# Recurrent chains in six phases a chunk that advance lane by lane in step, with TensorE's program in emission order in the second of two stretches

## The chip, the cores and the metric

The kernel runs on one core of a Trainium2 chip. The metric is the device time of one execution in microseconds (us); a smaller number is better. A profile gives for one execution each instruction's start and duration on the five engines: TensorE (PE, with its weight loads as PEld), VectorE (DVE), ScalarE (ACT), GpSimd (POOL) and SyncE (SP), which here issues nearly all DMAs.

## What is computed

One step of a hybrid backbone over 1152 tokens, 128 of context and 1024 latent, with model width 1024. A shared input projection feeds two parallel heads: a matrix-valued recurrence (RWKV-7: 8 heads of 64, both directions of time) and a gated linear recurrence (RG-LRU). Their outputs are concatenated, projected, gated and added; a gated feed-forward block with a width-3 convolution and a final norm follow. All vectors of shift, scale and gate come from a modulation product of the conditioning with `w_mod`. Cut to what the change concerns, of the reference:

```python
def _wkv7_step(S, inp):
    r_t, w_t, kk_t, b_t, k_t, v_t = inp
    sa = jnp.einsum('dbhij,dbhj->dbhi', S, kk_t)
    S = S * w_t[..., None, :] - sa[..., :, None] * b_t[..., None, :] + v_t[..., :, None] * k_t[..., None, :]
    y = jnp.einsum('dbhij,dbhj->dbhi', S, r_t)
    return S, y
...
mod = (jax.nn.silu(cvec) @ lp['w_mod'] + lp['b_mod'])[..., None, :]
...
x = x + g1 * (jnp.concatenate([ya, yb], axis=-1) @ lp['w_out'])
```

## The kernel before

**Chunks and lanes.** The matrix recurrence is done in chunks of 64 tokens. Two heads share one group f (0 to 3), and both directions of time go side by side. A chain (`chain`, L1100) carries the state of such a group through its tile positions p, two chunks (n_ = 0, 1) a position. For each chunk TensorE computes: keys and receptances times the state (KR by S, 128x128); G·V, the masked products of the chunk by the values (64x64 blocks); T·R, the triangular inverse times the right-hand side (64x64); K·V, the update of the state, and the second half of G·V (both 128x64). Between them ScalarE and VectorE copy the right-hand side R out of PSUM, write T·R into the values VS, add K·V to the state S and add the output o. `prep` (L1079) makes the next chunk's products: a 128x256 block product that VectorE masks into G (L1087), a scaling on GpSimd (L1090), and transposes (L1094) that ScalarE copies into Kt (L1095).

**Two stretches.** Four lanes carry the chains. Lanes a and b begin while the projection is still under way: the first stretch runs them beside `rest_of_projection` (L991), with the RG-LRU. Then memory is freed, and the second stretch runs the rest of a and b, lanes c and d (groups 0 and 1 from position 5 on), the normalisation of finished pieces (`post`, L1277, whose transposes are `po`), the rest of the modulation (`mod_rest`, L1335: sets of eight 128x512 tiles `wmod`, multiplied into PSUM tile `md` in 32-column pieces by `mod_part`, L315, then turned by `mod_cols`) and the RG-LRU half of the output projection (`wout_lru`, L1413: rounded weights `woh`, `wol`, products `wo`).

**Order.** `beside_all` takes its generators in proportion to given weights; the code emits instructions in that order. A scheduler then orders each engine's instructions: among those that it deems ready, the first emitted goes first. A chunk of a chain has three steps (three `yield`s). PSUM has eight banks; `deal` names the banks that a kind of product takes in turn, and a new product in a bank waits until the earlier one there has been read. For the second stretch:

```python
    two = (2, 4)
    deal(ya=(3,), yb=(5,), yc=(0,), yd=(1,), pa=two, pb=two, pc=two, pd=two, ca=two[::-1], cb=two[::-1], cc=two[::-1],
         cd=two[::-1], md=(6,), wo=(7,), po=two)
    run_all((lane_a, 98 - LA), (lane_b, 98 - LB), (lane_c, 26), (lane_d, 26), (posts(90), 90),
            (seq(mod_rest(16, 24), beside_all((mod_rest(24, 48), 30), (wout_lru(), 48))), FL))
```

Here p stands for the products of `prep`, c for T·R and K·V, y for the outputs. In the first stretch each of these has its own bank for a and for b. LA is 74, LB 52: the steps of a and b in the first stretch, 24 and 16.7 chunks.

Of the kernel before, what the change touches and what calls it, by code (L numbers as in the profile page):

```python
# [10 lines left out]
AF = mybir.ActivationFunctionType  # L11
# [6 lines left out]
NT = 9  # L18
# [3 lines left out]
SPAN = ((0, 384), (384, 768), (768, 1152))  # L22


LA = 74
NT4, NAB4, NAG, NP, NL4, NC2 = 2, 4, 10, 1, 6, 6
PK, PX, PU = 4, 2, 4
RA, RL, RI, RK = 4, 1, 3, 2
# [2 lines left out]
def beside_all(*gens):  # L31

    st = [[g, float(n), 0] for g, n in gens]
    while st:
        s = min(st, key=lambda e: e[2] / e[1])
        try:
            next(s[0])
            s[2] += 1
            yield
        except StopIteration:  # L40
            st.remove(s)

# [16 lines left out]
def tile_hybrid_step(  # L59
# [10 lines left out]
    load = nc.sync.dma_start  # L70
# [20 lines left out]
    def mm(out, lhsT, rhs, start=True, stop=True):  # L91
        PE.matmul(out, lhsT, rhs, start=start, stop=stop, skip_group_check=True)  # L92
# [25 lines left out]
    def half(i):  # L118
        return slice(64 * i, 64 * i + 64)
# [113 lines left out]
    n = 0  # L233
# [708 lines left out]
    class Background:  # L942


        def __init__(self):
            self.q, self.done = [], set()
# [5 lines left out]
        def step(self):  # L952
            if not self.q:
                return False
            try:
                next(self.q[0])
            except StopIteration:
                self.done.add(id(self.q.pop(0)))
            return True

        def finish(self, g=None):
            while self.q and (g is None or id(g) not in self.done):
                self.step()

    bg_a, bg_l, bg_i, bg_k, bg_p = [Background() for _ in range(5)]

    def beside(gens, *rates):
        credit = [0.0] * 4
# [58 lines left out]
    class Lane:  # L1027


        def __init__(self, pool, k, out=None):  # L1030
            self.out = out or pool
            self.pool, self.k, self.py, self.pc, self.pp = pool, k, "y" + k, "c" + k, "p" + k

        def ring(self, name, n, bufs=2):
            return self.pool.tile([128, n], F32, name=name, tag=name + self.k, bufs=bufs)

# [21 lines left out]
    def fetch_keys(L, q, n_):  # L1058

        cs = slice(128 * n_, 128 * n_ + 128)  # L1060
        bk = L.ring("BK", 256).rearrange("p (d t) -> p d t", d=2)
        load(bk, kb_d[q.f, q.p, :, :, 1, cs])
        if n_ == 1:
            for e in range(2):
                A.activation(L.kx[half(e), :, :, e, :], q.KR[half(e)], AF.Copy)
        q.X[n_] = bk, L.kx[:, :, n_]

    FO = 2
    WL = V
# [9 lines left out]
    def prep(L, q, n_):  # L1079

        gm = L.ring("G", 512).rearrange("p (d e t) -> p d e t", e=2, d=2)
        km = L.ring("Kt", 256)
        bk, kx = q.X.pop(n_)
        ps = bank(L.pp)
        for d in range(2):
            mm(ps[:, 256 * d:256 * d + 256], bk[:, d], kx[:, d].rearrange("p e t -> p (e t)"))
        V.tensor_tensor(gm, ps.rearrange("p (d e t) -> p d e t", e=2, d=2),  # L1087
                        mask[:, :, n_].unsqueeze(2).to_broadcast([128, 2, 2, 128]), op=OP.mult)
        x = 2 * q.p + n_
        G.tensor_tensor(bk, bk, pc_f[q.f][:, :, x:x + 1].to_broadcast([128, 2, 128]), op=OP.mult)  # L1090
        yield
        ps = bank(L.pp)
        for d in range(2):
            PE.transpose(ps[:, 128 * d:128 * d + 128], bk[:, d], ident)  # L1094
        A.activation(km, ps[:, 0:256], AF.Copy)  # L1095
        q.G[n_] = gm
        q.K[n_] = km.rearrange("p (d t) -> p d t", d=2)
        yield

    def chain(L, pairs):  # L1100

        ring, S_buf = [0], L.states()

        def next_state():
# [4 lines left out]
        qs = {0: fetch(L, *pairs[0])}  # L1109
        fetch_keys(L, qs[0], 0)  # L1110
        fetch_keys(L, qs[0], 1)
        yield from prep(L, qs[0], 0)
        Sc = None
        for hi, (i, n_) in enumerate(hops):
            f, p = pairs[i]
# [39 lines left out]
            py = bank(L.py)  # L1155
            for d in range(2):
                mm(py[:, 128 * d:128 * d + 128], q.KR[:, d, n_], Sc[:, d, :], d == 0, False)
            for e in range(2):
                for d in range(2):
                    vh = vhalf(n_, d)  # L1160
                    mm(py[half(1 - vh), 128 * d + 64 * e:128 * d + 64 * e + 64], q.G[n_][half(vh), d, e, half(1 - vh)],
                       q.V[half(vh), n_, d, half(e)], False, True)
# [10 lines left out]
            for d in range(2):  # L1173
                sh = half(1 - vhalf(n_, d))
                copy(use[d], q.V[sh, n_, d, :], ps[sh, 0:128])
            next(ahead, None)
            yield
            if not last:
                ps = bank(L.pc)
# [12 lines left out]
            for d in range(2):  # L1192
                vh = half(vhalf(n_, d))
                dst, src = o[vh] if p == 0 else o[vh, d if p < 5 else 1 - d], py[vh, 128 * d:128 * d + 128]
                if p > 4 or (p == 0 and n_ == 1):
                    V.tensor_tensor(dst, src, dst, op=OP.add)
                else:
                    A.activation(dst, src, AF.Copy)
            for _ in ahead:
                pass  # L1200
            yield
            if p == 0 and n_ == 1:
                ctx_final(L, f, Sc)
                if f % 2:
                    bg_p.push(late_post(None, f // 2, oX))
            elif p > 4 and n_ == 1:
                bg_p.push(late_post(f, p, o))
            elif n_ == 1:
                spill(o_d[f, 4 - p], o.rearrange("p d c -> p (d c)"))
                if p == 4 and (i + 1 == len(pairs) or pairs[i + 1] != (f, 5)):  # L1210
                    spill(s_d[f], Sc.rearrange("p d c -> p (d c)"))

    def late_post(f, p, o):
        yield from post(f, p, o)
# [10 lines left out]

    oX = rp.tile([128, 512], F32, name="oX")
    E, LATE = range(1, 5), range(5, NT)
    lane_a = chain(Lane(rp, "a"), [(0, p) for p in E] + [(f, 0) for f in range(4)] + [(2, p) for p in range(1, NT)])
    lane_b = chain(Lane(rp, "b"), [(1, p) for p in E] + [(3, p) for p in range(1, NT)])

    PB = 2
    TM = 3
# [3 lines left out]
    YB = 2  # L1236
    YS = 1
    XP = 2
    FL = 88
    XC = 3  # L1240
    OC = 3
    OB = 3
    LB = 52

    def take(g, n):
        for _ in range(n):
            next(g)
            yield

    run_all((take(lane_a, LA), LA), (take(lane_b, LB), LB), (rest_of_projection(), 12 + (54 - 6 * len(EARLY)) * 4 // PK))  # L1250
    ph.close()
    use[1] = A
    pqs = ExitStack()
# [8 lines left out]
    def of_output(name):  # L1262
        return pw if name in ("woh", "wol", "yb", "ybh", "ybl") else p3

    lane_c, lane_d = [chain(Lane(lcd, k, pq), [(f, p) for p in LATE]) for f, k in ((0, "c"), (1, "d"))]

    def p2(name, dt=F32, bufs=2):
        return of_output(name).tile([128, 512], dt, name=name, tag=name, bufs=bufs)
# [57 lines left out]
            spill(y_d[2 * p:2 * p + 2, :, 0:128].rearrange("f p t -> p f t"), gt)  # L1326
        yield

    def posts(n):
        for _ in range(n):  # L1330
            bg_p.step()
            yield


    def mod_rest(i0, i1):  # L1335
        for idx in range(i0, i1, 4):
            ps = bank("md")
            raw = []
            for k in range(8):
                raw.append(p2("wmod", bufs=6))  # L1340
                load(raw[k], ins["w_mod"][0, 128 * k:128 * k + 128, 128 * idx:128 * idx + 512])
                if k % 2:
                    yield
                if k % 4 == 3:
                    for i in range(k - 3, k + 1):
                        mod_part(ps, slice(0, 512), i, raw[i], True)
            row = p2("tm")
            A.activation(row, ps, AF.Copy)
            mod_cols(idx, row, 4)
            yield  # L1350

# [61 lines left out]
    def wout_lru():  # L1413
# [24 lines left out]
        for k in range(4):  # L1438
# [3 lines left out]
    two = (2, 4)  # L1442
    deal(ya=(3,), yb=(5,), yc=(0,), yd=(1,), pa=two, pb=two, pc=two, pd=two, ca=two[::-1], cb=two[::-1], cc=two[::-1],
         cd=two[::-1], md=(6,), wo=(7,), po=two)
    run_all((lane_a, 98 - LA), (lane_b, 98 - LB), (lane_c, 26), (lane_d, 26), (posts(90), 90),
            (seq(mod_rest(16, 24), beside_all((mod_rest(24, 48), 30), (wout_lru(), 48))), FL))
    bg_p.finish()
    p3x.close()
    lcds.close()
# [410 lines left out]
```

## Time and profile before

| | |
|---|---|
| median of 3 runs | 1852.57 us (1850.71 to 1853.16) |
| the profiled execution | 1849.17 us |
| its span, first to last instruction | 1847.5 us |
| busy in the span: TensorE, VectorE, ScalarE, GpSimd | 1716.4, 1272.2, 865.5, 721.8 us |
| mean granted TensorE clock | 0.954 of full speed |
| first stretch (lanes a, b beside the projection) | 468 to 737 us |
| second stretch (four lanes, modulation, half of the output projection) | 737 to 959 us |

Times in the rows are microseconds from the start of the span, unless a mean is given in ns. A 4-byte matmul stands as two records, one of the rounded kind as one. A row of the timeline gives start, duration, engine, line, operation, tile written and tiles read, shape of the array part and of the operand, and how many records it merges; a bracket gives idle time before it and what ended that. Matmuls overlap: the distance of two starts, not the duration, is what a matmul costs the engine.

### The profile page before, as it was taken

How to read it: one execution, taken by the hardware profiler on the slowest of the kernel's cores; microseconds unless marked ns; L12 is line 12 of the kernel's file. 1: busy time of each engine (PE TensorE's matmuls, PEld its weight loads, DVE VectorE, ACT ScalarE, POOL GpSimd, SP SyncE). 2: the span in 40 equal slices, each digit the busy share in tenths (PEclk: the TensorE clock that was granted, in tenths of full speed). 3: DMA queues.
4: the chain of work that ended last, by engine and by line, in shares of the span. 5: the costliest groups of instructions: out<-in, count | busy, mean ns of one | idle time of the engine just before them, and what ended most of it. 6: DMA issues, size and time to landing. Idle time of an engine off the chain costs nothing.

```text
span 1847.5 us, 35759 instructions
## 1 busy us (share of the span) xinstructions
PE 1716.4 (93%) x13341; PEld 1442.9 (78%) x13341; DVE 1272.2 (69%) x2633; ACT 865.5 (47%) x1787; POOL 721.8 (39%) x742
## 2 busy tenths in 40 slices
PE   5998898888999989899988789999999998999996
PEld 4776676678777778456656689999999998888885
DVE  5458967797477664476788877676767667576764
ACT  6466655643666756333335844444444443121211
POOL 1022423322355344131121166666666663434340
PEclk8898979889999999899999899999999999999998
DMA  9254544443443434867775222222222225558571
GB/s 300 63 163 155 174 139 135 147 147 118 145 122 97 131 104 146 257 194 231 232 254 189 82 64 86 78 72 72 74 79 75 77 73 171 184 159 262 173 252 57
DMA packets 268428, 264.92 MB, mean 143 GB/s; under 512 B 21173, under 2 KB 218448, under 8 KB 268256
## 3 DMA queue, kind: packets, MB, share of 16 engines
q1 hardware_dynamic: 252496, 245.97, 42.1%
q10 hardware_dynamic: 15472, 16.54, 2.7%
q8 instruction: 105, 1.72, 0.4%
q14 instruction: 67, 0.55, 0.1%
q0 software_dynamic: 288, 0.14, 0.0%
HBM read 188.00 MB, written 74.58 MB: 142 GB/s over the span
## 4 chain that ended last, share of the span: by engine, by line
PE 66%; DVE 9%; ACT 3%; DMA 3%; issue 3%; POOL 3%; SPq 0%; ACTq 0%; POOLq 0%; DVEq 0%
PE acc L92 14%; PE x L92 7%; PE y L92 7%; PE z L92 7%; PE mm L92 7%; PE v L92 3%; PE wo L92 3%; PE ya L92 2%; PE lg L92 2%; PE md L92 2%; PE pa L92 2%; PE ca L92 1%; DVE X L501 1%; PE yb L92 1%; DVE gt L499 1%
## 5 line engine op out<-in xcount | busy, mean ns | idle before, releaser
L92 PE MATMUL mm<-h_hi,winp 128*128 128x384 f32 x1056 | 304.4, 358 | 4.9 <-DVE vr L808 3.2
L92 PEld LDWEIGHTS mm<-h_hi,winp 128*128 128x128 f32 x1056 | 198.7, 196 | 26.4 <-issue 14.9
L92 PE MATMUL mm<-h_lo,winp 128*128 128x384 f32 x528 | 187.7, 356 | 3.0 <-DVE h_lo L112 3.0
L112 POOL TENSOR_TENSOR wl<-raw,wh 128x512 fp32r<-128x512 f32 x110 | 155.1, 1412 | 69.7 <-ACT wh L106 69.4
L106 ACT ACTIVATE wh<-raw 128x512 fp32r<-128x512 f32 x110 | 69.5, 633 | 148.3 <-PE z L92 81.0
L92 PE MATMUL x<-f_hi,wh 128*128 128x256 f32 (+1 forms) x352 | 105.8, 301 | 8.9 <-ACT q L1652 5.3
L92 PEld LDWEIGHTS mm<-h_lo,winp 128*128 128x128 f32 x528 | 103.7, 197 | 9.6 <-DVE h_lo L112 4.5
L1090 POOL TENSOR_TENSOR BK<-BK,pc 128x256 f32<-128x256 f32 x72 | 47.8, 664 | 150.5 <-PE pa L92 58.8
L92 PE MATMUL x<-f_lo,wh 128*128 128x256 f32 (+1 forms) x352 | 105.5, 300 | 0.2 <-DVE f_lo L112 0.2
L92 PE MATMUL y<-t_hi,wh 128*128 128x320 f32 (+1 forms) x352 | 104.9, 298 | 0.7 <-DVE q L1657 0.7
L92 PE MATMUL x<-f_hi,wl 128*128 128x256 f32 (+1 forms) x352 | 105.3, 299 | 0.0
L92 PE MATMUL y<-t_lo,wh 128*128 128x320 f32 (+1 forms) x352 | 104.7, 297 | 0.0
L92 PE MATMUL y<-t_hi,wl 128*128 128x320 f32 (+1 forms) x352 | 104.6, 297 | 0.0
L112 POOL TENSOR_TENSOR wl<-S,wh 128x512 fp32r<-128x512 f32 x44 | 57.7, 1311 | 105.6 <-ACT wh L106 105.6
L92 PE MATMUL acc<-f_hi 128*128 128x512 f32 x330 | 91.0, 397 | 3.2 <-ACT zf L1760 3.2
L108 POOL TENSOR_SCALAR t_hi<-raw 128x512 fp32r<-128x512 f32 x66 | 52.9, 804 | 81.6 <-PE acc L92 35.4
L1619 DVE SCALAR_TENSOR_TENSOR zf<-C,fcw,zf 128x567 f32<-128x567 f32 x66 | 63.5, 962 | 23.3 <-ACT zf L1617 23.3
L92 PEld LDWEIGHTS acc<-f_hi 128*128 128x128 f32 x330 | 63.1, 192 | 16.9 <-ACT zf L1760 3.7
L92 PEld LDWEIGHTS x<-f_hi,wh 128*128 128x128 f32 x352 | 67.9, 193 | 9.9 <-ACT q L1652 5.8
L112 DVE TENSOR_TENSOR t_hi<-raw,t_hi 128x512 fp32r<-128x512 f32 x66 | 48.1, 735 | 37.0 <-POOL t_hi L108 37.0
L1617 ACT ACTIVATE zf<-C,colB,fcw 128x576 f32<-128x576 f32 x66 | 57.3, 868 | 28.1 <-DVE C L1689 15.7
L600 POOL TENSOR_TENSOR kd<-kd,rk 128x512 f32<-128x512 f32 (+1 forms) x24 | 32.2, 1342 | 97.0 <-ACT kd L598 96.8
(516 smaller groups left out, 5211.1 us busy)
## 6 DMA issues: line engine op xcount, KB each, us to landing
raw<-in_w_down SPq DMA_DIRECT2D x132, 256.0 KB, 3.1
raw<-in_w_up SPq DMA_DIRECT2D x88, 256.0 KB, 3.0
wmod<-in_w_mod SPq DMA_DIRECT2D x68, 256.0 KB, 4.2
act_d<-zf SPq DMA_DIRECT2D x44, 288.0 KB, 2.2
src<-act_d SPq DMA_DIRECT2D x66, 192.0 KB, 3.8
win<-in_w_in SPq DMA_DIRECT2D x44, 256.0 KB, 3.9
KR<-kb_d SPq DMA_DIRECT2D x36, 256.0 KB, 3.2
VS<-v_d SPq DMA_DIRECT2D x36, 256.0 KB, 3.2
```

Source lines behind the costliest of these rows:

```text
L92: PE.matmul(out, lhsT, rhs, start=start, stop=stop, skip_group_check=True)
L106: A.activation(hi, src, AF.Copy)
L108: eng.tensor_scalar(hi, src, 1.0, 0.0, op0=OP.mult, op1=OP.add)
L112: eng.tensor_tensor(lo, src, hi.bitcast(F32), op=OP.subtract)
L499: V.tensor_tensor(tv, X[:, q + 1:32, q:q + 1].to_broadcast([128, m, q]), X[:, q:q + 1, 0:q].to_broadcast([128, m, q]), op=OP.mult)
L501: V.tensor_tensor(X[:, q + 1:32, 0:q], X[:, q + 1:32, 0:q], tv, op=OP.add)
L600: G.tensor_tensor(self.kd, self.kd, self.k, op=OP.mult)
L1090: G.tensor_tensor(bk, bk, pc_f[q.f][:, :, x:x + 1].to_broadcast([128, 2, 128]), op=OP.mult)
L1617: A.activation(u, src, AF.Identity, scale=fcw[:, 1, m:m + 1], bias=colb("ffn_conv_b", m))
L1619: V.scalar_tensor_tensor(dv[:, :, 1:64], sv[:, :, 0:63], fcw[:, 0, m:m + 1], dv[:, :, 1:64], op0=OP.mult, op1=OP.add)
```

## The change

Each chunk of a chain gets six phases, each ended by a `yield`: A, KR by S, and in the second stretch the block product of the next chunk's `prep` too; B, G·V and R; C, T·R and the copies into VS; D, that block product in the first stretch; E, K·V, state, second G·V and o; F, the transposes of `prep`, then the copies kx (`head_blocks`, which stood in `fetch_keys`), and posts. In the first stretch, a and b go through each phase together in two rounds of three, a alone in the third, 24 rounds, with the steps of the projection spread over phases D, E and F. In the second stretch, 17 rounds alternate between the pairs ab and cd half a chunk apart, inside a block in which TensorE's program keeps the order of emission; `mod_rest` asks for six tiles ahead and takes a step for each four of them; the first rows of `w_out` are asked for before all else; two posts advance at once. The banks are dealt as before.

```diff
@@ chain
-        yield from prep(L, qs[0], 0)
+        yield
+        head_blocks(L, qs[0])
+        for _ in prep(L, qs[0], 0):
+            pass
+        yield
...
                 mm(py[:, 128 * d:128 * d + 128], q.KR[:, d, n_], Sc[:, d, :], d == 0, False)
+            if L.ahead:
+                next(ahead, None)
+            yield
...
                 copy(use[d], q.V[sh, n_, d, :], ps[sh, 0:128])
-            next(ahead, None)
+            yield
+            if not L.ahead:
+                next(ahead, None)
             yield
...
+            yield
             for _ in ahead:
                 pass
-            yield
+            if n_ == 0 and i + 1 < len(pairs):
+                head_blocks(L, qs[i + 1])
...
+            yield
@@ Together, for bg_p
+        def step(self):
+            for g in self.q[:2]:
+                try:
+                    next(g)
+                except StopIteration:
+                    self.q.remove(g)
+            return bool(self.q)
@@ first stretch
-    run_all((take(lane_a, LA), LA), (take(lane_b, LB), LB), (rest_of_projection(), 12 + (54 - 6 * len(EARLY)) * 4 // PK))
+    class Feed:
...
+        def turn(self, part=1.0):
+            self.credit += self.share * part
+            while self.credit >= 1.0:
+                self.credit -= 1.0
+                next(self.g, None)
...
+    def phase(lanes):
+        for g in lanes:
+            next(g, None)
+
+    in_order = {mybir.EngineType.PE}
+    rest = Feed(rest_of_projection(), NREST, 24)
+    if True:
+        phase((lane_a, lane_b))
+        phase((lane_a, lane_b))
+        for r in range(24):
+            lanes = (lane_a, lane_b) if r % 3 < 2 else (lane_a,)
+            for ph_ in "ABCDEF":
+                phase(lanes)
+                if ph_ in "DEF":
+                    rest.turn(1.0 / 3.0)
+        rest.finish()
@@ mod_rest
+        ask(6)
+        yield
         for idx in range(i0, i1, 4):
             ps = bank("md")
-            raw = []
-            for k in range(8):
-                raw.append(p2("wmod", bufs=6))
-                load(raw[k], ins["w_mod"][0, 128 * k:128 * k + 128, 128 * idx:128 * idx + 512])
-                if k % 2:
-                    yield
-                if k % 4 == 3:
-                    for i in range(k - 3, k + 1):
-                        mod_part(ps, slice(0, 512), i, raw[i], True)
+            for k0 in (0, 4):
+                for i in range(4):
+                    mod_part(ps, slice(0, 512), k0 + i, raw[i], True)
+                del raw[:4]
+                yield
+                ask(4)
             row = p2("tm")
             A.activation(row, ps, AF.Copy)
+            yield
             mod_cols(idx, row, 4)
             yield
@@ second stretch (FL is now 83, NREST 70)
-    run_all((lane_a, 98 - LA), (lane_b, 98 - LB), (lane_c, 26), (lane_d, 26), (posts(90), 90),
-            (seq(mod_rest(16, 24), beside_all((mod_rest(24, 48), 30), (wout_lru(), 48))), FL))
+    for L in (la, lb, lc_, ld_):
+        L.ahead = True
+    of_lru = wout_lru()
+    next(of_lru)
+    late = Feed(seq(mod_rest(16, 24), beside_all((mod_rest(24, 48), 24), (of_lru, 48))), FL, 17)
+    with tc.manual_schedule(engines=in_order):
+        ab, cd = (lane_a, lane_b), (lane_c, lane_d)
+        phase(cd)
+
+        for h in range(17):
+            x, y = (ab, cd) if h % 2 == 0 else (cd, ab)
+            late.turn(1.0 / 3.0)
+            bg_p.step()
+            if h > 1:
+                phase(x)
+            elif h == 1:
+                phase(cd)
+            late.turn(1.0 / 3.0)
+            bg_p.step()
+            if h < 16:
+                phase(x)
+            late.turn(1.0 / 3.0)
+            if h > 0:
+                phase(y)
+            bg_p.step()
+            if h < 16:
+                phase(x)
+            if h > 0:
+                phase(y)
+                phase(y)
+        phase(cd)
+        late.finish()
```

## Rows read from the trace of the kernel before

**Rows 1.** The page, its first line.
```profile
span 1847.5 us, 35759 instructions
```

**Rows 2.** Busy time by stretch; counts of instructions in brackets, then granted clock, DMA share, GB/s.
```profile
468.00:705.00 237.00, 227.19 (x2137) 180.13 (x2137) 155.64 (x322) 157.63 (x328) 103.47 (x112) 0.98 0.38 115
...
806.00:959.00 153.00, 152.23 (x1259) 102.97 (x1260) 116.48 (x338) 55.63 (x160) 28.11 (x42) 1.00 0.74 237
...
737.00:959.00 222.00, 208.64 (x1685) 135.67 (x1686) 151.20 (x438) 80.99 (x226) 44.84 (x66) 0.96 0.72 232
```

**Rows 3.** Timeline of TensorE from 865 us: three groups of one shape, and the next shape.
```profile
865.21 0.45 PE L92 MATMUL yb<-VS,G 128*64 128x64 f32 x8
865.49 0.40 PE L92 MATMUL ca<-VS,Kt 128*64 128x64 f32 x8
865.72 0.40 PE L92 MATMUL ya<-VS,G 128*64 128x64 f32 x8
866.06 0.44 PE L1094 MATMUL pa<-ident,BK 128*128 128x128 f32 x2
```

**Rows 4.** Timeline of TensorE: the first and the last runs of the second stretch.
```profile
743.63 2.05 PE L92 MATMUL pc<-kxc,BK 128*128 128x256 f32 x4 [6.76 <-DMA BK<-kb_d]
...
956.54 1.06 PE L92 MATMUL md<-wmod,silx 128*32 128x512 f32 x8
957.53 0.44 PE L1321 MATMUL po<-ident,osq 128*128 128x128 f32 x2
```

**Rows 5.** TensorE by shape, 737 to 959 us; then the timeline around a short md run.
```profile
L92 PE MATMUL md<-wmod,silx 128*32 128x512 f32 x128 | 35.4, 617 | 0.0
...
868.77 1.05 PE L92 MATMUL md<-wmod,silx 128*32 128x512 f32 x2
869.75 1.13 PE L92 MATMUL pc<-kxc,BK 128*128 128x256 f32 x4
```

**Rows 6.** Timeline of TensorE: successive products of lanes c and d in one bank.
```profile
867.13 0.45 PE L92 MATMUL cc<-R,TTp 64*64 64x64 f32 x8
...
868.40 0.45 PE L92 MATMUL cd<-R,TTp 64*64 64x64 f32 x8
...
825.82 0.38 PE L1094 MATMUL pc<-ident,BK 128*128 128x128 f32 x2
826.04 0.39 PE L92 MATMUL yb<-S1b,KR 128*128 128x128 f32 x2
...
826.73 0.44 PE L1094 MATMUL pd<-ident,BK 128*128 128x128 f32 x2
...
932.13 1.13 PE L92 MATMUL pc<-kxc,BK 128*128 128x256 f32 x4
933.19 0.45 PE L92 MATMUL cd<-R,TTp 64*64 64x64 f32 x8
...
934.37 1.03 PE L92 MATMUL pd<-kxd,BK 128*128 128x256 f32 x4
...
849.12 0.45 PE L92 MATMUL cc<-VS,Kt 128*64 128x64 f32 x8
...
850.42 0.45 PE L92 MATMUL cd<-VS,Kt 128*64 128x64 f32 x8
```

**Rows 7.** Groups of ScalarE and VectorE, 737 to 959 us: busy us, mean ns, idle before.
```profile
L1075 ACT ACTIVATE VS<-cc 64x128 f32<-64x128 f32 x16 | 4.3, 272 | 4.3 <-PE cc L92 4.1
...
L1408 DVE TENSOR_TENSOR tm<-wo,g1b 128x512 f32<-128x512 f32 x18 | 12.4, 688 | 4.6 <-PE wo L92 4.3
```

**Rows 8.** The head of the second stretch: timeline, busy time, DMA issues of 737 to 959 us.
```profile
751.46 1.79 PE L92 MATMUL md<-wmod,silx 128*32 128x512 f32 x4
...
743.00:751.00 8.00, 5.86 (x14) 3.49 (x14) 2.87 (x6) 2.03 (x4) 1.23 (x2) 0.50 1.07 346
...
wmod<-in_w_mod SPq DMA_DIRECT2D x64, 256.0 KB, 4.0
```

**Rows 9.** Busy time by stretch, in the first stretch.
```profile
660.00:670.00 10.00, 8.17 (x64) 6.25 (x64) 7.66 (x16) 3.25 (x9) 3.74 (x6) 0.66 0.29 84
```

More of the change, by code (lines that the diff above doesn't have):

```diff
@@ L22 @@
 SPAN = ((0, 384), (384, 768), (768, 1152))
-LA = 74
+NREST = 70
 NT4, NAB4, NAG, NP, NL4, NC2 = 2, 4, 10, 1, 6, 6
@@ L963, in finish @@
                 self.step()
-    bg_a, bg_l, bg_i, bg_k, bg_p = [Background() for _ in range(5)]
+    class Together(Background):
+        def step(self):
[5 more added lines that the diff above has]
+            return bool(self.q)
+    bg_a, bg_l, bg_i, bg_k = [Background() for _ in range(4)]
+    bg_p = Together()
     def beside(gens, *rates):
@@ L1032, in __init__ @@
             self.pool, self.k, self.py, self.pc, self.pp = pool, k, "y" + k, "c" + k, "p" + k
+            self.ahead = False
         def ring(self, name, n, bufs=2):
@@ L1062, in fetch_keys, with head_blocks @@
         load(bk, kb_d[q.f, q.p, :, :, 1, cs])
-        if n_ == 1:
-            for e in range(2):
-                A.activation(L.kx[half(e), :, :, e, :], q.KR[half(e)], AF.Copy)
         q.X[n_] = bk, L.kx[:, :, n_]
+    def head_blocks(L, q):
+        for e in range(2):
+            A.activation(L.kx[half(e), :, :, e, :], q.KR[half(e)], AF.Copy)
     FO = 2
@@ L1227, in tile_hybrid_step @@
     E, LATE = range(1, 5), range(5, NT)
-    lane_a = chain(Lane(rp, "a"), [(0, p) for p in E] + [(f, 0) for f in range(4)] + [(2, p) for p in range(1, NT)])
-    lane_b = chain(Lane(rp, "b"), [(1, p) for p in E] + [(3, p) for p in range(1, NT)])
+    la, lb = Lane(rp, "a"), Lane(rp, "b")
+    lane_a = chain(la, [(0, p) for p in E] + [(f, 0) for f in range(4)] + [(2, p) for p in range(1, NT)])
+    lane_b = chain(lb, [(1, p) for p in E] + [(3, p) for p in range(1, NT)])
     PB = 2
@@ L1238, in tile_hybrid_step @@
     XP = 2
-    FL = 88
+    FL = 83
     XC = 3
@@ L1243, in tile_hybrid_step, with __init__, finish @@
     LB = 52
-    def take(g, n):
-        for _ in range(n):
-            next(g)
-            yield
-    run_all((take(lane_a, LA), LA), (take(lane_b, LB), LB), (rest_of_projection(), 12 + (54 - 6 * len(EARLY)) * 4 // PK))
+    class Feed:
+        def __init__(self, g, n, turns):
+            self.g, self.share, self.credit = g, n / turns, 0.0
+        def turn(self, part=1.0):
[3 more added lines that the diff above has]
+                next(self.g, None)
+        def finish(self):
+            for _ in self.g:
+                pass
+    def phase(lanes):
[13 more added lines that the diff above has]
+        rest.finish()
     ph.close()
@@ L1263, in of_output @@
         return pw if name in ("woh", "wol", "yb", "ybh", "ybl") else p3
-    lane_c, lane_d = [chain(Lane(lcd, k, pq), [(f, p) for p in LATE]) for f, k in ((0, "c"), (1, "d"))]
+    lc_, ld_ = [Lane(lcd, k, pq) for k in "cd"]
+    lane_c, lane_d = [chain(L, [(f, p) for p in LATE]) for f, L in ((0, lc_), (1, ld_))]
     def p2(name, dt=F32, bufs=2):
@@ L1327, in post, with ask @@
         yield
[L1329 to L1332, printed above, removed]
     def mod_rest(i0, i1):
+        todo = [(idx, k) for idx in range(i0, i1, 4) for k in range(8)]
+        raw = []
+        def ask(n):
+            for idx, k in todo[:n]:
+                raw.append(p2("wmod", bufs=6))
+                load(raw[-1], ins["w_mod"][0, 128 * k:128 * k + 128, 128 * idx:128 * idx + 512])
+            del todo[:n]
+        ask(6)
+        yield
         for idx in range(i0, i1, 4):
             ps = bank("md")
-            raw = []
-            for k in range(8):
-                raw.append(p2("wmod", bufs=6))
-                load(raw[k], ins["w_mod"][0, 128 * k:128 * k + 128, 128 * idx:128 * idx + 512])
-                if k % 2:
-                    yield
-                if k % 4 == 3:
-                    for i in range(k - 3, k + 1):
-                        mod_part(ps, slice(0, 512), i, raw[i], True)
+            for k0 in (0, 4):
[4 more added lines that the diff above has]
+                ask(4)
             row = p2("tm")
             A.activation(row, ps, AF.Copy)
+            yield
             mod_cols(idx, row, 4)
```

## The prediction, made before the changed kernel was run

> **What bounds the kernel now.** I read the page first, then busy time by stretch, then TensorE's instructions by shape, then the timeline of the stretch that the change rewrites, and last the SyncE queue. The page says a span of 1847.5 us [rows 1]; the profiled execution took 1849.2 us, 1.7 us more than its span, and 3.4 us less than the median of the three runs, 1852.6 us. I add to 1849.2 and give the answer on the median.
>
> The change touches two stretches. The first, from 468 to 737 us, has lanes a and b beside the rest of the projection: TensorE is busy 227.2 us of the 237 up to 705 us. The second, 737 to 959 us, has four lanes beside the modulation (md) and the recurrent half of the output projection (wo): TensorE is busy 208.6 of 222 us, and 152.2 of the last 153 us [rows 2]. VectorE is busy 151.2 of those 222 us and the DMA engines 72%. So in both stretches TensorE is the bound, and what counts is how its instructions follow one another.
>
> Within that busy time there are two losses. **Changes of shape.** Three groups of eight small records in one shape (yb, ca, ya) start 0.28 and 0.23 us apart, and the next shape comes 0.34 us after the last [rows 3]. So leaving a shape costs about 0.10 us, and starting a run of a 64-column shape about 0.04 more. In the timeline from 743.63 to 957.53 us I count 238 runs of one shape (the first and the last are in [rows 4]). **Split md runs.** An md matmul uses 32 columns; four that follow each other lie side by side. A run of two records (one matmul) takes 0.98 us up to the next shape [rows 5], a run of eight 0.99 [rows 4]. The 128 records are busy 35.4 us [rows 5] in 33 runs, 17 of them of two records, the first at 751.46, the last at 956.54 us [rows 4, 8].
>
> **The change, part by part.** *The order of the second stretch.* I walk through the new loop: in each of 17 rounds TensorE gets full-width work (wo, the transposes of phase F, then KR times state and the block product of phase A), then T·R of one pair and G·V of the other, both 64x64, then K·V and G·V, both 128x64. That is three changes of shape a round; the 16 md blocks add about 28 and the post transposes that fall between T·R and G·V in six rounds about 12. Counted out: 87 runs, 151 fewer, of them 65 fewer runs of a 64-column shape: 151 x 0.10 + 65 x 0.04 = 17.7 us off, at half of that if the planner's order was already cheap where the records interleave. *md in fours:* 33 runs become 16: 17 x 0.98 = 16.7 us off. Together **-34 us** (bounds -20 and -40).
>
> *What emission order adds.* Until now, whenever TensorE's next chain group could not start, the planner put wo or md in its place. In emission order nothing passes a waiting matmul, and two lanes in step ask for the same thing one behind the other. The deal of PSUM banks is unchanged: pa to pd all alternate over banks 2 and 4, ca to cd over 4 and 2. Lanes a and b, and c and d, now advance at the same phase, so both lanes of a pair draw the same bank at each step, and the second lane's group waits until the first's is read out. Four times a round:
> - T·R, bank 4: the second may start when two VS copies of 0.272 us [rows 7] are done. The trace has cc and cd 1.27 us apart; a group in a run takes 0.23: 1.04 us of waiting.
> - Transposes of phase F, bank 4: a Kt copy on ScalarE stands between. pc and pd are 0.91 us apart, the first's own two records take 0.22: 0.69 us.
> - Block product, bank 2: VectorE's masked G. pc and pd stand 2.24 us apart; the first's own records take 1.06 less a change of shape, 0.96, and the second lane's KR product (four records of 0.11, as the transposes) goes beside it, 0.45: 0.83 us, or about 0.5 if VectorE is idle at that moment.
> - K·V, bank 2: two state sums on VectorE. cc and cd stand 1.30 us apart, 0.46 of it covered by K·V and G·V (two groups of 0.23): 0.84 us.
>
> The distances are those of [rows 6], for each kind the shortest between lanes c and d, which draw the same bank before the change too. That makes 3.4 us a round; with 15 full rounds **+50 us** (35 to 58). The distance is there before as well, but other matmuls fill it. In the six rounds with two posts the second transpose shares bank 4 with T·R as well: 6 x 0.8 = +5.
> The Trainium skill (Perfetto Trace Analysis, Optimizing Tensor Performance, Matmuls) wants independent matmul groups to rotate through PSUM banks so that reading out one overlaps the next. By that rule the change puts neighbours in one bank where it should part them; with them parted the sum below would be 50 us less. Rows 6 agree with it.
>
> *wo and md have one bank each.* A half-row of wo ends in a VectorE product of 0.688 us [rows 7], and the next half-row's first matmul waits for it. 18 such places, about 1 us each, most covered by chain phases in between: +4 (0 to 10).
>
> *The head of the second stretch.* The first md comes at 751.46 us, 14 us after the stretch begins; TensorE has work from 743, 5.9 us of it in the 8 us before, at a granted clock of 0.50, that is 1.2 GHz [rows 8]. After that the planner gives it whatever has landed. In the new order eight w_out loads (three at once, three buffers) and the fetches of c and d come ahead of the first six wmod loads, and md is the first thing in TensorE's line. Its second block of four needs two tiles that are asked for only when the first block has freed its buffers, then a load of 4.0 us median [rows 8] behind everything SyncE has already put on the queue (the DMA engines are fully busy, share 1.07, from 743 to 751 us). The third and fourth block do the same. Three waits of 5 to 10 us in line, with some 10 us of lane work between them that must itself wait behind md: 13 to 35 us, I take **+25**, since the queue is full there and each wait is nearer to 8 than to 5. Behind the waiting md stand lanes a and b, whose work is ready.
>
> *Posts two at a time, kx copies moved to phase F, the loads of w_mod asked earlier:* the same instructions on engines with room (ACT is busy 81 of 222 us [rows 2]): 0; if ACT's cover goes, two kx copies stand in front of VS in every second round, within the range above.
>
> *The first stretch* stays with the planner. Lane a does the same 24 chunks, lane b 16 instead of 16.7, and the remaining steps of the projection are spread over all rounds, instead of leaving a tail of bare projection after the lanes. TensorE has 9.8 us idle in 468 to 705 to lose. 16 rounds now offer two lanes' groups next to each other; if half of lane b's 80 groups join a neighbour at 0.14 us each: -6 (bounds -16 and +5, since the planner may still split them, and waits of two lanes now coincide).
>
> Sum: -34 + 50 + 5 + 4 + 25 - 6 = +44; 1849.2 + 44 = 1893 us, on the median **1897 us**.
>
> **Rivals.** *Faster, the same mechanism decided the other way:* the waits for banks 2 and 4. If the readers come so early that a round waits only 1 us, and the head costs 8: -34 - 6 + 17 + 8 = -15, 1838 us. It decides at 40 us of waiting in all, 2.3 us a round. For it: TensorE is busy 152.2 of 153 us, so each saved change counts fully. Against it: rows 6 have no pair of this kind closer than I used. Beside this rival stands the Trainium skill (TensorEngine Tiling (Array Packing), Key Properties): changing the tiling mode drains the engine. Rows 3 show that drain as 0.10 us; by that rule alone the change could only gain. Chance 0.16.
> *The head alone:* rounds cost 1 us, but the md waits reach 35 us: -34 - 6 + 16 + 4 + 35 = +15, 1868 us. For it: the full queue of rows 8. Chance 0.10.
> *The clock:* with TensorE at work about 9 of 13 us a round, the granted clock falls. It was 0.66 from 660 to 670 us, with TensorE busy 8.2 of 10 [rows 9]. Half clock in a third of the 175 us left adds 58: 1955 us. Against: the single waits are about 1 us. Chance 0.07.
> *It doesn't do what it says:* the planner's order stays in effect the old one: 1847 to 1853 us, chance 0.04.
>
> **How the numbers follow.** The forecast has 0.63. Slower by over 0.2% (3.7 us, about what a measurement of this kernel can tell) is 0.63 + 0.10 + 0.07 = 0.80; within it 0.04; faster 0.16. The forecast alone spans 1857 to 1945 by its bounds (not all at one end). For 8 in 10 I go from 1848, which takes in no change, to 1950; most of the faster rival and of the clock's lie outside.
>
> **What would show it.** Right: about 87 shape runs and 16 md runs of eight records in the stretch; TensorE's busy time there down by about 30 us yet the stretch some 50 us longer; the waits of cb and cd on VS copies, of pb and pd on G, and of pb and pd on Kt among its longest; in the first 50 us, md waiting on wmod loads. Wrong: second lanes that start 0.3 us after the first, or a stretch shorter than 222 us; then the banks were not the bound. A first stretch that moves by over 16 us would also fall outside the working.

## The result, and the profile after

| | before | after |
|---|---|---|
| median of 4 runs | 1852.87 us (1850.71 to 1855.38) | 1908.07 us (1903.37 to 1910.07) |
| the profiled execution, its span | 1849.17, 1847.5 us | 1910.07, 1908.4 us |
| mean granted TensorE clock | 0.954 | 0.931 |

The changed kernel is slower by a ratio of 1.0287 [1.0261, 1.0313], 55.2 us by the medians. The forecast was 1897 us, "slower" with a chance of 0.80; 1908 lies in the range of 1848 to 1950. Its sum was +44 us.

Where the 60.9 us between the two spans arose is read from four marks that both traces have: the first block product of lane a, the transpose of `lru_fin` that ends the first stretch, the first transpose `tr` that follows the second, and the end. Busy time by stretch, cut at these marks, before:

```profile
459.19:736.61 277.42, 265.37 (x2360) 213.47 (x2360) 169.90 (x344) 181.96 (x372) 123.75 (x130) 0.98 0.40 124
736.91:960.20 223.29, 209.14 (x1689) 136.09 (x1689) 152.44 (x443) 81.08 (x226) 45.46 (x67) 0.96 0.73 232
```

and after (the columns of [rows 2]: PE, PEld, DVE, ACT, POOL busy with counts, clock, DMA share, GB/s):

```profile
462.74:750.85 288.11, 265.76 (x2294) 215.66 (x2294) 171.50 (x339) 178.66 (x363) 120.24 (x127) 0.92 0.38 117
751.15:1020.12 268.97, 205.11 (x1755) 143.33 (x1755) 155.99 (x453) 83.50 (x239) 47.18 (x73) 0.87 0.62 201
```

The lanes start 3.5 us later, the first stretch takes 10.7 us longer, the second 45.7, and what follows 1.0: 60.9 in all. In the second stretch TensorE is busy 4.0 us less and idle 63.9 us where it was idle 14.2, so these rows show the loss as waiting. But the clock fell from 0.96 to 0.87 as well, and busy time at half clock is longer, so the rows alone do not say what the waits cost and what the clock cost. Counted by shape as in the prediction, the 238 runs have become 86 and the 33 runs of md 15 (two of the 16 md blocks follow each other): the change did what it says.

TensorE's waits in the second stretch after the change (what waited, its releaser; us in total, times, longest):

```profile
PE md L92 <- issue: 10.1, 1, 10.1
PE md L92 <- DMA wmod<-in_w_mod: 7.0, 3, 3.6
PE cb L92 <- ACT VS L1090: 5.6, 8, 0.9
PE cd L92 <- ACT VS L1090: 5.4, 8, 0.8
PE pd L1109 <- ACT Kt L1110: 4.7, 7, 1.3
PE pb L1109 <- ACT Kt L1110: 4.3, 7, 0.8
PE pb L92 <- DVE G L1102: 3.7, 7, 1.6
PE pd L92 <- DVE G L1102: 3.1, 6, 0.9
...
PE yd L92 <- DMA S1d<-s_d: 2.1, 1, 2.1
...
PE yc L92 <- DMA S1c<-s_d: 1.8, 1, 1.8
```

Those of the second lanes b and d for VS, Kt, G and, in four rows not shown, for the state sums of K·V (8.2 us) add up to 35.0 us; the head (md, yc, yd) has 21.0. The timeline shows both. Second lanes of a pair, after the change:

```profile
820.28 0.45 PE L92 MATMUL cc<-R,TTp 64*64 64x64 f32 x8
821.38 0.27 PE L92 MATMUL cd<-R,TTp 64*64 64x64 f32 x2 [0.65 <-ACT VS L1090]
...
837.09 0.45 PE L92 MATMUL ca<-VS,Kt 128*64 128x64 f32 x8
838.39 0.45 PE L92 MATMUL cb<-VS,Kt 128*64 128x64 f32 x8 [0.62 <-DVE S0a L1212]
...
841.89 0.38 PE L1109 MATMUL pa<-ident,BK 128*128 128x128 f32 x2
842.83 0.41 PE L1109 MATMUL pb<-ident,BK 128*128 128x128 f32 x2 [0.56 <-ACT Kt L1110]
...
844.42 1.03 PE L92 MATMUL pa<-kxa,BK 128*128 128x256 f32 x4
846.23 1.13 PE L92 MATMUL pb<-kxb,BK 128*128 128x256 f32 x4 [0.34 <-DVE G L1102]
```

Start to start that is 1.10, 1.30, 0.94 and 1.81 us. The head:

```profile
761.24 2.52 PE L92 MATMUL md<-wmod,silx 128*32 128x512 f32 x4 [10.12 <-issue]
767.40 2.59 PE L92 MATMUL md<-wmod,silx 128*32 128x512 f32 x4 [3.64 <-DMA wmod<-in_w_mod]
771.62 2.85 PE L92 MATMUL md<-wmod,silx 128*32 128x512 f32 x4 [1.63 <-DMA wmod<-in_w_mod]
776.17 2.60 PE L92 MATMUL md<-wmod,silx 128*32 128x512 f32 x4 [1.70 <-DMA wmod<-in_w_mod]
778.70 1.23 PE L92 MATMUL ya<-S0a,KR 128*128 128x128 f32 x4
```

The first two md blocks come in four halves, one after the other. Three of them wait for a load of `wmod`; for the 10.1 us before the first the view names no releaser. From 761 to 779 us the granted clock is 0.50, and a half, four records, takes 2.5 us and more, where eight records took 1.06 at full clock [rows 4]. Lane a's `ya` behind them, whose work was ready, starts 28 us after the stretch began.

### The profile page after: what moved, and what is told of

It is laid out like the page before. It is cut to its first block, busy times and chain, and to the rows that moved or that the text cites. A ratio compares the mean times of both kernels' runs of the same rounds, so it can differ in the third digit from the quotient of the medians.

```text
span 1908.4 us, 35786 instructions
## 1 busy us (share of the span) xinstructions
PE 1718.8 (90%) x13341; PEld 1457.1 (76%) x13341; DVE 1272.3 (67%) x2631; ACT 862.5 (45%) x1789; POOL 719.8 (38%) x742
## 4 chain that ended last, share of the span: by engine, by line
PE 46%; DVE 5%; ACT 2%; DMA 2%; issue 1%; POOL 1%; SPq 0%; DVEq 0%; ACTq 0%; POOLq 0%
PE acc L92 13%; PE x L92 7%; PE y L92 7%; PE z L92 7%; PE v L92 3%; PE wo L92 2%; PE mm L92 2%; PE md L92 1%; DMA v<-v_d 1%; POOL wl L112 1%; ACT VS L1090 0%; DVE G L1102 0%; PE pd L92 0%; DVE tm L1471 0%; DVE o L1223 0%
## 5 line engine op out<-in xcount | busy, mean ns | idle before, releaser
L92 PE MATMUL mm<-h_hi,winp 128*128 128x384 f32 x1056 | 309.8, 362 | 4.0 <-DVE vr L808 2.5
L92 PEld LDWEIGHTS x<-f_lo,wh 128*128 128x128 f32 x352 | 68.2, 194 | 0.5 <-DVE f_lo L112 0.4
```

## The experiments

All edits are to the changed kernel unless said otherwise. The comparison with the kernel before was repeated beside each group; its medians were 1854.9, 1853.7 and 1853.3 us.

**e1_planner: the order alone undone.**

```
-    with tc.manual_schedule(engines=in_order):
+    if True:
```

> Only the emission order goes: the planner orders TensorE in the second stretch too; phases, md in fours, deal of banks and first stretch stay as changed. Theory A (in emission order the second lane's wait for its bank, 35.0 us of TensorE's waits in all, and the head's 21 us stand uncovered): the planner puts other matmuls in their place, the shape changes come back in part (about 10 us), the first stretch keeps its loss: 1860 to 1875 us, waits for VS, Kt, G and the state sums together under 10 us. Rival (the step itself is the cost, whoever orders TensorE, since two lanes ask for the same engine at the same moment): above 1895 us.

Measured: 1873.68 us (1.0103 [1.0075, 1.0131]), 34.4 below the changed kernel. TensorE's waits in its second stretch, the three largest of the second lanes':

```profile
PE cd L92 <- ACT VS L1090: 1.6, 4, 0.4
...
PE pb L92 <- DVE G L1102: 1.4, 2, 1.1
PE pd L92 <- DVE G L1102: 1.2, 1, 1.2
```

4.2 us in place of 12.2 for the same three rows; TensorE is busy 216.9 us, 11.8 more, in some 200 runs of one shape. The planner fills the waits and pays with changes of shape, as Theory A had it.

**e2_banks: the shared banks alone undone.**

```
- pb=two, pd=two, cb=two[::-1], cd=two[::-1]
+ pb=two[::-1], pd=two[::-1], cb=two, cd=two
```

> Emission order and everything else kept; lanes b and d draw banks 2 and 4 in the opposite turn to a and c, so the two lanes of a pair no longer meet in one bank. Theory A (the bank is what the second lane waits for): of the 35.0 us of waits for VS, Kt, G and the state sums at least 25 go, 1875 to 1885 us. Rival (what is waited for is the chain itself, the bank is beside the point): the same waits under other names, 1900 to 1912 us.

Measured: 1868.48 us (10 runs; 1.0086 [1.0053, 1.0119]), 39.6 us less, more than Theory A said. The waits of the second lanes for VS, G and the state sums are gone from the rows; the first lanes wait instead, and the posts, which still share banks 2 and 4:

```profile
PE po L1379 <- ACT VS L1090: 5.9, 6, 1.0
...
PE cc L92 <- ACT VS L1090: 4.9, 7, 0.7
```

```profile
457.93:735.74 277.81, 257.51 (x2293) 210.07 (x2294) 170.97 (x338) 178.57 (x363) 121.50 (x127) 0.96 0.40 121
736.04:967.79 231.75, 183.37 (x1754) 131.68 (x1755) 153.92 (x453) 81.70 (x239) 48.17 (x73) 0.93 0.73 234
```

TensorE runs the same instructions in the same order as in the changed kernel, and is busy 183.4 us in the second stretch, not 205.1. So idle time fell by 15.5 us and busy time by 21.7, with the clock at 0.93 instead of 0.87. This execution is the shortest of its ten runs (1858.15 us; the median is 10 us above), so its rows are read for kinds of waits, and the size from the medians.

**e7_before_banks: the same edit on the kernel before.**

> The kernel before, with nothing but the turn of the banks of lanes b and d reversed. Theory A (the planner fills a wait for a bank with other matmuls, TensorE being busy 152.2 of 153 us): no difference, 1848 to 1858 us. Rival (lanes c and d, which share a bank at each step in the kernel before, hold each other up there too): 1835 to 1845 us.

Measured: 1856.75 us (1.0023 [1.0003, 1.0043]), no gain. With the planner's order in the kernel before, the shared bank cost nothing. **e6_planner_banks** joins e1 and e2:

> Both the emission order and the shared banks go: the planner orders TensorE, and lanes b and d draw the banks in the opposite turn. Theory A (order and banks cost only together: the planner had filled the bank's waits already, and keeps its many changes of shape): 1864 to 1874 us, as e1_planner. Rival (the shared bank costs the planner too, 5 us or more): 1850 to 1862 us.

Measured: 1865.41 us (1.0072 [1.0045, 1.01]), 8.3 us below e1_planner and 3.1 below e2_banks. It lies in the range of Theory A, but not for Theory A's reason: the 8.3 us are more than the 5 us at which the rival begins, and the runs of the two kernels do not overlap (1864.25 to 1867.73, against 1872.37 to 1875.81). So with the lanes in step the shared bank costs something under the planner too. Each edit alone brings most of what both bring.

**e4_head: no md in the first two rounds.**

```
-    late = Feed(seq(mod_rest(16, 24), beside_all((mod_rest(24, 48), 24), (of_lru, 48))), FL, 17)
+    late = Feed(seq(mod_rest(16, 24), beside_all((mod_rest(24, 48), 24), (of_lru, 48))), FL - 1, 15)
...
+        def turn(h):
+            if h > 1:
+                late.turn(1.0 / 3.0)
...
-            late.turn(1.0 / 3.0)
+            if h == 0:
+                next(late.g)
+            turn(h)
```

> In the first two rounds of the second stretch no md or wo stands in TensorE's line; their steps are spread over the 15 rounds that follow, and the first six loads of w_mod are asked where they were. Theory A (the head costs because lanes a and b stand behind an md that waits for its loads: 10.1 and 7.0 us of waits, and 10 us of md at half clock): ya starts by 755 us instead of 778.7 and the run is 12 to 20 us shorter, 1888 to 1896 us. Rival (the loads bound the head whatever stands in front, or md and wo then lack as cover for the waits later): 1903 to 1912 us.

Measured: 1901.56 us (1.0233 [1.0188, 1.0278]), 6.5 us less: neither theory's range. Lane a's `ya` does start at 752.66 us, but the line stops at the next things that need a load (`osq` is made from a tile `v`, whose load is issued at 769.04 us, behind those of w_out):

```profile
775.71 0.66 PE L1379 MATMUL po<-ident,osq 128*128 128x128 f32 x2 [10.78 <-DVE osq L1375]
...
785.18 1.23 PE L92 MATMUL yc<-S1c,KR 128*128 128x128 f32 x4 [7.21 <-DMA S1c<-s_d]
```

**e5_banks_loads: parted banks, the loads of w_out and w_mod asked one round later, and no md or wo in the first two rounds, as in e4_head.** Of its edit:

```
-    next(of_lru)
...
+            if h == 1:
+                next(late.g)
+                next(of_lru)
```

> The parted banks of e2_banks, and a head without the first loads of w_out and w_mod: both are asked for at the start of the second round instead of ahead of the first, md and wo stand in TensorE's line from the third round on. Theory A (the head is a queue of loads: w_out and w_mod stand before the data of the posts and of lanes c and d, and whatever is first in TensorE's line waits, md in the changed kernel, a post and S1c in e4_head): the waits of the first 50 us fall from 22 us in e2_banks to under 10, 1848 to 1860 us. Rival (md and wo, pressed into 15 rounds, give back what the head gains): 1864 to 1874 us, as e2_banks.

Measured: 1868.39 us (1.0082 [1.0053, 1.011]), as e2_banks. The rival had the number, but not the cause: by far the longest wait of TensorE is for one load, and the SyncE queue shows what stood ahead of it.

```profile
775.64 1.22 PE L92 MATMUL yc<-S1c,KR 128*128 128x128 f32 x4 [19.64 <-DMA S1c<-s_d]
```

```profile
765.78 1.94 SPq L1444 DMA_DIRECT2D wm<-in_w_out  x3
...
769.81 2.25 SPq L1444 DMA_DIRECT2D wm<-in_w_out  x2
...
772.59 0.61 SPq L1156 DMA_DIRECT2D S1c<-s_d  x1
```

The first three w_out loads were issued at 757.91 us; the other five wait for one of three buffers, and the load of lane c's state is behind them in the same queue. The queue's own waits for these buffers come to 4.5 us, so they explain only part of the 19.6: 14 loads of 256 KB (six of w_mod, eight of w_out) go ahead of the 128 KB that TensorE needs.

**e3_first and e8_pace: the first stretch.** In e3_first the lanes are no longer in step there; e8_pace also gives the projection its old pace:

```
-        for r in range(24): ... phase(lanes) ... rest.turn(1.0 / 3.0)
+    run_all((take(lane_a, 146), 146), (take(lane_b, 98), 98), (rest_of_projection(), NREST))   # e3_first
+    run_all((take(lane_a, 146), 146), (take(lane_b, 98), 98), (rest_of_projection(), 48))      # e8_pace
```

> Only the first stretch is undone: lanes a and b and the rest of the projection advance side by side, each at its own rate, as before the change (lane b with 16 chunks), not in step by phases. The second stretch stays as changed. Theory A (two lanes in step stop together when VectorE is in its long scans, up to 4.4 us a time, and the clock falls to 0.5 behind it; the projection no longer fills): the stretch ends at 737 to 742 us instead of 750.9, the run at 1894 to 1900 us. Rival (the loss lies in the six phases and the lane steps left beside the last gate work, not in the step): it ends near 750 us, 1905 to 1911 us.

Measured: 1907.47 us (1.0282 [1.0247, 1.0318]), no difference, the stretch 290.6 us long at a clock of 0.92. Going in step is not what costs there.

> As e3_first, with the one thing of the first stretch that e3_first left changed: the projection advances 48 of its 70 steps while the lanes do theirs, as before the change, and its last 22 follow by themselves. Theory A (the pace is what cost the first stretch: the lanes' last steps stand alone beside the gate work at its end): the stretch ends by 742 us, 1895 to 1901 us. Rival (neither step nor pace; the stretch is as long as its stalls behind VectorE and the clock after them): it ends near 750 us, 1902 to 1912 us.

Measured: 1897.2 us (1.0231 [1.019, 1.0273]), 10.9 us less than the changed kernel and 10.3 less than e3_first. The size is loose: four runs each, 1890.96 to 1907.03 against 1903.37 to 1910.07. Its two stretches:

```profile
470.67:744.80 274.13, 261.01 (x2295) 210.02 (x2294) 166.63 (x337) 182.60 (x366) 118.91 (x128) 0.98 0.41 126
745.10:1015.37 270.27, 198.43 (x1755) 141.87 (x1755) 155.55 (x455) 84.78 (x240) 46.80 (x72) 0.89 0.62 197
```

It ends at 744.8 us, not by 742, because in this execution the lanes began 8 us later; it is 274.1 us long instead of 288.1. The five profiles with the pace of 48 have 272.7 to 276.4 us there, the seven with 70 (the changed kernel's among them) 277.8 to 290.6, 9.8 us more on the average. So it is the pace.

**e9_all and its three variants.** e9_all joins e2_banks, e8_pace and a head without md or wo in the first two rounds, in which the w_mod loads are asked in the second round and those of w_out in the fourth; e10 to e12 change one thing each from it.

> Parted banks (e2_banks), the pace of the first stretch as before the change (e8_pace), and the head with the loads of w_mod asked in the second round and those of w_out in the fourth. Theory A (the eight w_out loads, which wait for three buffers, hold up the S1c load behind them: 19.6 us of wait in e5_banks_loads): 1868.5 us of e2_banks less about 11 for the pace and 12 to 18 for the head, 1838 to 1848 us, below the kernel before; the waits of the first 50 us of the second stretch under 8 us. Rival (another load stands in front next, and the clock falls at the head all the same): 1852 to 1862 us.

Measured: 1846.66 us (12 runs; 0.9967 [0.9951, 0.9984]): below the kernel before. The waits of the head did not fall under 8 us: a BK load and S1c hold it for 7.4 and 7.3.

```profile
737.23:958.83 221.60, 177.04 (x1722) 128.61 (x1723) 152.76 (x453) 79.27 (x232) 46.72 (x70) 0.93 0.76 241
```

```profile
PE pc L92 <- DMA BK<-kb_d: 7.4, 1, 7.4
PE yc L92 <- DMA S1c<-s_d: 7.3, 1, 7.3
PE po L1374 <- ACT VS L1090: 6.3, 6, 1.4
PE cc L92 <- ACT VS L1090: 4.9, 7, 0.7
```

The second lanes now follow at once, as in its timeline:

```profile
801.00 0.44 PE L1109 MATMUL pa<-ident,BK 128*128 128x128 f32 x2
801.27 0.38 PE L1109 MATMUL pb<-ident,BK 128*128 128x128 f32 x2
...
812.54 0.45 PE L92 MATMUL cc<-VS,Kt 128*64 128x64 f32 x8 [0.70 <-ACT VS L1090]
...
813.05 0.40 PE L92 MATMUL cd<-VS,Kt 128*64 128x64 f32 x8
```

> As e9_all, but with all lanes' banks in the turn of the changed kernel. Theory A (the shared bank is worth 35 us of waits and the clock that falls in them, whatever the head and the first stretch do): 35 to 45 us above e9_all. Rival (part of the 39.6 us between the changed kernel and e2_banks came from the head, where the waits overlapped): 20 to 30 us above it.

Measured: 1878.51 us (1.015 [1.0115, 1.0186]), 31.9 us above e9_all, between the two ranges. That is the shared bank by itself, once head and pace are mended. And it is 18.7 us below e8_pace: the head by itself, with the banks shared.

```profile
737.11:986.20 249.09, 187.73 (x1723) 132.75 (x1723) 153.13 (x453) 80.95 (x232) 45.71 (x70) 0.93 0.67 213
```

> As e9_all, with the planner's order of TensorE in the second stretch. Theory A (with the waits away, emission order is worth its fewer changes of shape, 26 us of busy time between e6_planner_banks and e2_banks): 8 to 20 us above e9_all. Rival (the planner has shorter waits to the same amount): within 4 us of e9_all.

Measured: 1854.16 us (1.0002 [0.9986, 1.0017]), 7.5 us above e9_all, just under Theory A's range and outside the rival's. TensorE is busy 203.2 us there, 26.2 more, in 154 runs of one shape instead of 86 and 40 runs of md instead of 16; it is idle 23.6 us instead of 44.6. So emission order is worth something once its waits are away, and most of what it saves in busy time it still loses in waits.

> As e9_all, with the transposes of the posts in the bank of wo (7) instead of banks 2 and 4 by turns. Theory A (the 5.9 us that po waits for VS copies in e2_banks are the shared bank once more): 4 to 6 us below e9_all. Rival (po waits for the readers of wo instead, 0.69 us each): within 3 us of e9_all or above it.

Measured: 1848.03 us (0.9964 [0.9946, 0.9982]), as e9_all: po now waits 6.0 us for VectorE's product `gd`, which reads the po before it out of the one bank.

## Why the prediction was right, and where not

Three steps between measured kernels take the changed kernel back: the pace 10.9 us (to e8_pace, which also gives up going in step, worth nothing by e3_first), the head 18.7 (to e12_order_shared), the banks 31.9 (to e9_all). That is 61.4; less the 6.2 us by which e9_all lies below the kernel before (at 1852.87) it is the 55.2 of the result. The parts depend on the order of the steps: taken first, the banks are 39.6 (to e2_banks), and pace and head together 21.8 (to e9_all) in place of 29.6.

**The gain of -34 was there.** 86 runs against 87 worked out, 15 runs of md against 16. Busy time of the second stretch is 209.1 us before and 177.0 in e9_all: 32.1 less. (The 66 records of lane b that the change moves into this stretch are in it, and some 33 of lanes a and b fall just ahead of its border in e9_all: 33 more than before.) But the trace of the changed kernel doesn't show it: its busy time is only 4.0 us lower, for two reasons given under the clock. "TensorE's busy time there down by about 30 us" was wrong as a sign to look for; the other signs (runs of one shape, the second lanes' waits, md behind its loads) came. And little of the gain reaches the end: e9_all is idle 44.6 us there, the kernel before 14.2.

**The banks, +50.** The mechanism was right, in its four places and by its readers. The distances of [rows 6] were 1.27, 0.91, 2.24 and 1.30 us; the changed kernel has medians of 1.10 (T·R), 1.00 (transposes), 1.81 (block product) and 1.31 (K·V). With banks parted (e2_banks) they are 0.28, 0.22, 1.31 and 0.51. The differences are 0.82, 0.78, 0.50 and 0.80, 2.9 us a round, 43.5 in 15 rounds against 50. The block product (0.83 in the prediction) and T·R (1.04) were the terms too large. The end moved by less, 31.9 us, or 39.6 with the old head: where the second lane no longer waits, other groups wait for their own chain (cc for VS 4.9 us, which no row of the changed kernel's waits has, and the posts 4.5 us more than in e12_order_shared). The term was taken as if all of it came back; that step is too dear by a fifth to a third. The 5 us for posts behind T·R were not there while the lanes waited anyway (1.4 us) and came up with the banks parted (6.3 us).
The rule of the Trainium skill that the prediction weighed against the change (Perfetto Trace Analysis, Optimizing Tensor Performance, Matmuls: independent groups in turn through PSUM banks) is borne out here by 31.9 to 39.6 us in emission order; the 50 us that the prediction set on it were too many. With the planner's order it was worth 8.3 us where the lanes go in step (e6_planner_banks) and nothing in the kernel before (e7_before_banks).

**The head, +25.** The changed kernel waits 21.0 us there, and mending the loads gave 18.7. The reason given, w_out and w_mod loads ahead of all else on SyncE, held; that md is what stands in front did not matter by itself (e4_head, 6.5 us). What matters is what stands ahead in the load queue, bulk loads and among them loads that wait for a buffer, and that in emission order any one late tile stops all lanes.

**The first stretch, -6, is the step that failed.** "The remaining steps of the projection are spread over all rounds, instead of leaving a tail of bare projection after the lanes" was counted as free. Undoing it gives about 10 us (10.9 by the medians, 9.8 by the profiles of the stretch). The whole term was -6, with bounds of -16 and +5, and came out at +10.7, outside them, in the two executions compared. That one pair is not firm: the stretch took 277.8 to 288.1 us in the six profiles with the changed kernel's first stretch, and 277.4 and 280.8 in the two with the old one (the kernel before, e7_before_banks), on the average 282.6 and 279.1. What is firm is that the gain did not come. With the old pace it is 272.7 to 276.4, so a gain of the hoped-for size was there without the new pace.

What makes the new pace dear is not shown. In the changed kernel's first stretch two VS copies stand behind scans of the RG-LRU on VectorE, and TensorE waits for them, 8.6 us in all; here one of them, with the 10 us that follow:

```profile
520.00:530.00 10.00, 5.62 (x38) 4.23 (x38) 7.09 (x7) 4.34 (x8) 8.05 (x4) 0.87 0.17 52
530.00:540.00 10.00, 9.87 (x66) 7.30 (x65) 8.37 (x15) 4.74 (x11) 6.90 (x5) 0.62 0.13 41
```

TensorE runs dry, then works at a lower clock. But e3_first, with the new pace and no step, has 3.1 us of these waits and is no shorter, so these two waits are not the whole cause. What does go with the length is the clock: 0.92 in the changed kernel and in e3_first, 0.98 in e8_pace. In the whole stretch TensorE is idle 22.4 us (288.1 less 265.8) in the changed kernel, 13.1 in e8_pace.

**wo and md, +4:** the waits for tm and g1b come to 3.0 us. **The clock** had a chance of 0.07 for 1955 us, and entered the sum nowhere. It fell from 0.96 to 0.87 in the second stretch. The truth lay between the two cases: e2_banks, with the same program on TensorE, has 21.7 us less busy time, nearly all of it after the first 60 us. The changed kernel, then e2_banks:

```profile
811.15:1020.12 208.97, 170.12 (x1569) 123.86 (x1569) 133.38 (x395) 68.66 (x206) 35.14 (x54) 0.94 0.58 186
796.04:967.79 171.75, 148.87 (x1543) 113.21 (x1542) 131.23 (x395) 66.30 (x203) 35.96 (x54) 0.99 0.70 224
```

Two things can make up the difference. The first belongs to the bank waits themselves: a group that the next one follows at once shares its last 0.17 us with it (T·R lasts 0.45 us, the next starts after 0.28), and one that stands alone does not. At four places in each of 15 rounds that is an estimate of 10 us, and e12_order_shared has in fact 10.7 us more busy time than e9_all at the same mean clock. The second is the clock. If a mean of 0.94 stands for full and half clock mixed, 12% of 209 us are at half clock, against 2% of 172 at 0.99; half of that time is lost if half the clock does half the work, so this is an estimate of up to 11 us. Why the rounds after 870 us fell to a lower clock in the changed kernel's execution but hardly in e12_order_shared's, is open.

So the total came out within 11 us in part by luck. The banks, the head and the first stretch (+50, +25 and -6, together +69) came to 61.4. What is left (-34, +5 and +4, together -25) came to -6.2, by which e9_all, with the three taken away, lies below the kernel before. Costs too high by 8 and a gain too high by 19 set each other off in part; and within the 61.4 the first stretch had the wrong sign and the clock had no term.

## What to carry to other kernels

When an engine's order is fixed by hand, every wait that a planner used to fill stands open, so look first at what two neighbours in that order share: a PSUM bank, a buffer ring, a load queue. Part the banks of what runs side by side, and ask for the data of the first rounds before bulk loads that must wait for buffers. Fewer changes of shape are worth their price only after that: here 32 us of busy time became 6 us at the end.

## What had not been expected of the hardware

The same program on TensorE takes different times, and they go with its clock. In the changed kernel and in e2_banks the first stretch has the same order of instructions on TensorE and the same longest waits (ca for VectorE's VS copies, 8.6 us in each), and took 288.1 us at a mean clock of 0.92 and 277.8 at 0.96. The four other profiles with this first stretch lie in the same line: 287.5 us at 0.92, 281.6 and 281.1 at 0.94, 279.6 at 0.96. So part of the 10.7 us by which this stretch grew between the two executions compared can be the clock of the one execution. The ten runs of e2_banks go from 1858.15 us (clock 0.951 over the span) to 1878.73 (0.937).

One scan of VectorE had twice its usual length, and it set one of those long waits:

```profile
524.56 2.73 POOL L904 TENSOR_TENSOR a<-a,th 128x1152 f32<-128x1152 f32 x1
524.80 4.63 DVE L911 TENSOR_TENSOR_SCAN th<-th,colA,a 128x1024 f32<-128x1024 f32 x1
529.47 0.29 DVE L1092 COPY VS<-ca 64x128 f32<-64x128 f32 x1
```

Of the eight such scans of this trace seven took 2.3 to 2.6 us. GpSimd was at work on a 128x1152 product for 2.5 us of the long one, and the scan ends 2.15 us after that product, a little under its usual length. In the kernel before it is the other way round: a scan from 649.74 us takes its usual 2.33, and a product that begins beside it is the long one:

```profile
649.89 4.64 POOL L904 TENSOR_TENSOR a<-a,th 128x1152 f32<-128x1152 f32 x1 [0.52 <-ACT a L901]
```

In the traces of the two kernels and of e2, e7, e8 and e9 two such instructions overlap eight times by more than 0.3 us, and each time the one that begins second ends 2.14 to 2.15 us (a scan) or 2.45 to 2.47 us (a product) after the end of the first, as if it had waited for the first. No run was made to test it.
